# Sparse attention in units of two: scores of both, two half dense products with a transposition each, then the values of both

## Chip, cores and metric

The kernel runs on one core of a Trainium2 chip. The metric is the device time of one execution in microseconds (us), as a median of several.

## What is computed

Two networks of two layers each, on 512 tokens of width 1024. The first network mixes tokens by a gated linear recurrence and by sparse attention, whose three branches (compressed, selected, window) are gated and summed; the second has convolution, retention, spatial gating, cross attention and a feed-forward part. Only the selected and the window branch of the first network are at issue. With 512 tokens both are causal attention over all keys, since 16 blocks of 64 tokens, or a window of 512, cover the whole sequence:

```python
o_slc = selected_attn(q_rope, k_sl, heads(vsl, KVH), sel, scale)
o_win = window_attn(q_rope, k_wn, heads(vwn, KVH), scale)
gates = jax.nn.sigmoid(ngate).reshape(B, T, 3, KVH, G).transpose(2, 0, 3, 4, 1)[..., None]
o_nsa = gates[0] * o_cmp + gates[1] * o_slc + gates[2] * o_win
y_nsa = o_nsa * jax.nn.silu(nz)
h = h + jnp.concatenate([y_hg, y_nsa], axis=-1) @ w_out[i]
```

There are 8 query heads of width 64, handled in 4 pairs j, and 4 tiles t of 128 query rows.

## The kernel before

Dense products run on TensorE in float32 split into a high and a low part: `acc_fm` (line 458) issues three matmuls of 512 columns for each of 8 tiles of 128 inputs (lines 463 to 465), the weights' high part `whi` made on ScalarE (line 425), the low part `wlo` on VectorE or GpSimd (line 427). The raw weights come by DMA on SyncE's queue. `lin_steps` yields between the first and the last 12 matmuls of such a product: a dense half. `first_fill` (line 751) is a generator of such halves: the gates nz, hgo and hz (tanh `th` on ScalarE, line 784, a multiplication on VectorE, line 789), then the per-layer products wpp (`pp`, line 865), with small steps of the compressed branch (`Sc`, `ptc`) and of the recurrence (`spr`, `O`, line 1166) between them. Splits of activations into high and low parts (`yh`, `yl`, `ph`, `pl`) are lines 510 and 511. `pump(n)` runs n steps of the generator, and `pump(99)` what is left.

`nsa_pairs` (line 1298) does the two branches with an order of TensorE's instructions that is written out by hand, while the scheduler places the instructions of the other engines. A unit is a pair j, a tile t and one or both branches; n = 128(t+1) keys. There are 24 units in a layer, six for each j: t = 3 for each branch, t = 2 for each branch, then t = 1 and t = 0 with both branches at once. Each unit has three parts:

- `probs`: for each of the two heads a PSUM bank S, six score matmuls (line 1317) and two masks (line 1319); on VectorE the row maxima (line 1326) and their product with the scale (line 1328); on ScalarE exp with a running sum (line 1333); then the reciprocal of the sums and the gate (lines 1337 to 1341), and the scale of P on VectorE for one head (line 1343) and on ScalarE for the other (line 1344).
- `turn`: transposes of P on TensorE into a bank pt for each head (line 1356), copied to PT by ScalarE (line 1361) for one head and by VectorE (line 1363) for the other.
- `values`: matmuls of PT with v into the bank "no" of the pair (line 1376); with t = 0 also the compressed branch (lines 1379 and 1380), after which VectorE multiplies the sum by its gate (line 1382), and it is split.

S, pt, no, spr, Sc and ptc share six PSUM banks (`XB`); the dense products have two (`LIN`). Step i of the loop (line 1391 on) issues the scores and masks of unit i, the transposes of unit i-2, a dense half where `APUMP[i]` (line 1112) is 1, and the values of unit i-3. `APUMP` has 0 at i = 8, 14 and 19. At the end `begin` issues the first 21 matmuls of the output product wout.

Of the kernel before, what the change touches and what calls it, by code (L numbers as in the profile page):

```python
# [339 lines left out]
class Kern:  # L340
# [768 lines left out]
        self.pump()  # L1109

    DEEP = 2
    APUMP = tuple(map(int, "1111111101111101111011111"))
    HPUMP = (1,) * 16

    def stat_cols(self, ps, sq, o, rhs):
# [182 lines left out]
    def nsa_pairs(self, l, begin):  # L1298

        nc = self.nc  # L1300
        mm = nc.tensor.matmul
        po = [None]

        def probs(j, t, bs):

            ts = slice(t * 128, (t + 1) * 128)
            n = 128 * (t + 1)
            nb = len(bs)
            nm, sm = self.small([128, 2, 2], "nm", bufs=4), self.small([128, 2, 2], "sm", bufs=4)
            Ss = [self.xbank("S") for _ in range(2)]  # L1310
            bb = slice(bs[0], bs[-1] + 1)
            os = [S[:, :nb * n].rearrange("p (b s) -> p b s", b=nb) for S in Ss]
            qh, ql = self.q1[j]

            for i, (x, k) in enumerate(((qh, self.kh), (ql, self.kh), (qh, self.kl))):
                for o, hs in zip(os, HALVES):
                    mm(o, lhsT=x[hs, ts], rhs=k[hs, bb, :n], start=i == 0, stop=False)
            for o in os:
                mm(o[:, :, n - 128:], lhsT=self.identb, rhs=self.c["causal"][:, None, :].to_broadcast([128, nb, 128]),
                   start=False, stop=True)  # L1320
            Ps = {}
            rq = self.rq[:, j, t]

            with self.tc.high_priority(offset=200):
                for hd in range(2):
                    nc.vector.tensor_reduce(nm[:, :nb, hd], Ss[hd][:, :nb * n].rearrange("p (u s) -> p u s", u=nb),
                                            axis=AX, op=OP.max, negate=True)
                nc.vector.tensor_tensor(nm[:, :nb], nm[:, :nb], rq[:, None, :].to_broadcast([128, nb, 2]), op=OP.mult)  # L1328
                for hd in range(2):
                    P = self.slot("P")  # L1330
                    for i, b in enumerate(bs):
                        c = slice(i * n, i * n + n)
                        nc.scalar.activation(P[:, c], Ss[hd][:, c], AF.Exp, scale=rq[:, hd:hd + 1], bias=nm[:, i, hd:hd + 1],  # L1333
                                             accum_out=sm[:, i, hd:hd + 1])
                        Ps[b, hd] = P[:, c]
                s = sm[:, :nb]
                nc.vector.tensor_scalar(s, s, 1e-30, 4.0, op0=OP.max, op1=OP.mult)
                nc.vector.reciprocal(s, s)
                o = j * 6 + 2 + bs[0] * 2
                g = self.gth[:, t, o:o + nb * 2].rearrange("p (b h) -> p b h", h=2)  # L1340
                nc.vector.scalar_tensor_tensor(s, g, 1.0, s, op0=OP.add, op1=OP.mult)
                for i, b in enumerate(bs):
                    nc.vector.tensor_scalar(Ps[b, 0], Ps[b, 0], sm[:, i, 0:1], None, op0=OP.mult)
                    nc.scalar.activation(Ps[b, 1], Ps[b, 1], AF.Copy, scale=sm[:, i, 1:2])
            return Ps

        def turn(t, bs, Ps):

            n = 128 * (t + 1)
            PTs = []  # L1350
            for hd in range(2):
                pt = self.xbank("pt")
                for k, b in enumerate(bs):
                    for i in range(t + 1):
                        s = slice(i * 128, (i + 1) * 128)
                        nc.tensor.transpose(pt[:, k * n + i * 128:k * n + (i + 1) * 128], Ps[b, hd][:, s], self.ident)
                PT = self.slot("PT")
                m = len(bs) * n
                with self.tc.high_priority(offset=200):
                    if hd:  # L1360
                        nc.scalar.activation(PT[:, :m], pt[:, :m], AF.Copy)
                    else:
                        nc.vector.tensor_copy(PT[:, :m], pt[:, :m])
                PTs.append(PT)
            return PTs

        def values(j, t, bs, PTs):
            ts = slice(t * 128, (t + 1) * 128)
            n = 128 * (t + 1)
            if t == TT - 1 and bs[0] == 0:  # L1370
                po[0] = self.xbank("no")
            for k, b in enumerate(bs):
                for i in range(t + 1):
                    for hd in range(2):
                        v = self.vt[i][:, b * 128 + hd * 64:b * 128 + hd * 64 + 64]
                        mm(po[0][hd * 64:hd * 64 + 64, ts], lhsT=v, rhs=PTs[hd][:, k * n + i * 128:k * n + (i + 1) * 128],
                           start=t == TT - 1 and b == 0 and i == 0, stop=False)
            if t == 0:
                mm(po[0], lhsT=self.vc[0], rhs=self.pc[j], start=False, stop=False)
                mm(po[0], lhsT=self.vc[1 + j % 2], rhs=self.pc[j], start=False, stop=True)  # L1380
                O = self.slot("on")
                nc.vector.tensor_tensor(O, po[0], self.nzg[j], op=OP.mult)
                self.yn.append(self.split(O, "y"))

        branches = [((0, 1),), ((0, 1),), ((0,), (1,)), ((0,), (1,))]
        units = [(j, t, bs) for j in range(4) for t in reversed(range(TT)) for bs in branches[t]]
        n = len(units)
        Ps = {}


        with self.tc.manual_schedule(engines={mybir.EngineType.PE}):
            PTs = {}
            for i in range(n + 3):
                if i < n:
                    Ps[i] = probs(*units[i])
                if 0 <= i - 2 < n:
                    PTs[i - 2] = turn(*units[i - 2][1:], Ps.pop(i - 2))
                if i <= n:
                    self.pump(self.APUMP[i])
                elif i == n + 1:  # L1400
                    self.pump(99)
                    begin()
                if i >= 3:
                    values(*units[i - 3], PTs.pop(i - 3))


    def second(self, l):
# [491 lines left out]
```

## Time and profile before

| | |
|---|---|
| median of 3 runs | 2663.74 us (2661.94 to 2664.14) |
| the profiled execution | 2664.12 us, span 2662.4 us |
| granted TensorE clock, mean | 0.997 |
| TensorE, VectorE, ScalarE, GpSimd busy | 99%, 58%, 43%, 19% |
| the chain that ended last | TensorE 92%, VectorE 5%, ScalarE 2% |
| the attention stage of layer 0, of layer 1 | 211 to 351 us, 649 to 790 us |

The engines' shares are means over a span with several stages. The list of waits says for what TensorE stood still, the timeline gives single instructions with their starts, so that a start less the start before it is the pitch; the ends of matmuls are modelled. Windows give the busy time of each engine in a stretch, and the clock that TensorE was granted there (1.00 is full).

### The profile page before, as it was taken

Reading aid. Unit: us, or ns where it says so; the run is one execution under the profiler, and the core shown is the slowest. Engines: PE = TensorE matmul, PEld = TensorE weight load, DVE = VectorE, ACT = ScalarE, POOL = GpSimd, SP = SyncE. Lnnn points to the kernel's source line nnn. Section 1 sums busy time; section 2 is a strip of 40 time slices with the busy share of each in tenths; the row PEclk is TensorE's granted clock in tenths of the full one; section 3 lists DMA queues with packets and bytes.
Section 4 is the critical chain, followed back from the end, with each engine's and each line's share of the span. In section 5 each row is a group of like instructions: output and inputs, shape, how many; then the busy total and the mean of one; then the engine's idle time right before and its main releaser. Section 6 shows DMA issues by size and latency. Waiting matters only on the chain.

```text
span 2662.4 us, 34660 instructions
## 1 busy us (share of the span) xinstructions
PE 2629.0 (99%) x13574; PEld 2187.3 (82%) x13574; DVE 1537.1 (58%) x2310; ACT 1138.8 (43%) x2017; POOL 498.7 (19%) x430
## 2 busy tenths in 40 slices
PE   9999999999999999999999999999999999999998
PEld 7897778888778888888888888888888888888887
DVE  6687657687665655545555443555555555544444
ACT  5666655575664533334443222343333444422223
POOL 1254311054421141211010000114111000100101
PEclk9999999999999999999999999999999999999999
DMA  4311123321113323334323333232333432333332
GB/s 168 110 41 48 48 72 103 102 67 49 48 55 95 97 78 106 100 95 127 111 72 95 95 94 102 92 107 81 94 104 95 127 119 64 95 95 97 94 100 88
DMA packets 71890, 241.79 MB, mean 91 GB/s; under 512 B 8496, under 2 KB 11824, under 8 KB 71728
## 3 DMA queue, kind: packets, MB, share of 16 engines
q1 hardware_dynamic: 70288, 234.86, 28.8%
q0 software_dynamic: 1440, 4.72, 0.5%
q8 instruction: 108, 1.77, 0.3%
q14 instruction: 54, 0.44, 0.0%
HBM read 237.45 MB, written 2.10 MB: 90 GB/s over the span
## 4 chain that ended last, share of the span: by engine, by line
PE 92%; DVE 5%; ACT 2%; issue 1%; POOL 0%; DMA 0%; SPq 0%; DVEq 0%; ACTq 0%; POOLq 0%
PE lin_w L464 9%; PE lin_w L463 9%; PE lin_w L465 9%; PE lin_xq L464 1%; PE lin_wpg L464 1%; PE lin_xq L465 1%; PE lin_ga L465 1%; PE lin_ga L463 1%; PE lin_wo L463 1%; PE lin_wy L463 1%; PE lin_gc L463 1%; PE lin_gb L463 1%; PE lin_xq L463 1%; PE lin_wy L465 1%; PE lin_gc L465 1%; PE lin_gb L465 1%
## 5 line engine op out<-in xcount | busy, mean ns | idle before, releaser
L425 ACT ACTIVATE whi<-wraw 128x1024 fp32r<-128x1024 f32 (+2 forms) x433 | 453.1, 1047 | 1081.9 <-issue 531.5
L427 DVE TENSOR_TENSOR wlo<-wraw,whi 128x1024 fp32r<-128x1024 f32 (+2 forms) x409 | 562.8, 1377 | 155.1 <-ACT whi L425 150.8
L465 PE MATMUL lin_w<-xh,wlo 128*128 128x512 f32 x704 | 273.9, 389 | 0.0
L464 PE MATMUL lin_w<-xl,whi 128*128 128x512 f32 x704 | 273.9, 389 | 0.0
L463 PE MATMUL lin_w<-xh,whi 128*128 128x512 f32 x704 | 273.9, 389 | 0.0
L1519 POOL TENSOR_TENSOR fa<-fa,fb 128x512 f32<-128x512 f32 x44 | 61.1, 1389 | 613.7 <-DVE fb L610 510.4
L463 PEld LDWEIGHTS lin_w<-xh,whi 128*128 128x128 f32 x704 | 132.1, 188 | 27.6
L464 PEld LDWEIGHTS lin_w<-xl,whi 128*128 128x128 f32 x704 | 132.1, 188 | 27.4
L465 PEld LDWEIGHTS lin_w<-xh,wlo 128*128 128x128 f32 x704 | 132.1, 188 | 27.4
L464 PE MATMUL lin_w<-fyl,whi 128*128 128x512 f32 (+1 forms) x366 | 139.9, 382 | 0.9 <-DVE fyl L511 0.9
L463 PE MATMUL lin_w<-fyh,whi 128*128 128x512 f32 (+1 forms) x366 | 139.6, 381 | 0.0
L465 PE MATMUL lin_w<-fyh,wlo 128*128 128x512 f32 (+1 forms) x366 | 139.4, 381 | 0.0
L610 DVE TENSOR_TENSOR fb<-lin_w,rs 128x512 f32<-128x512 f32 x44 | 30.4, 691 | 138.9 <-PE lin_w L465 138.9
L1333 ACT ACTIVATE P<-S,nm,qkst 128x512 f32<-128x512 f32 (+3 forms) x128 | 77.6, 615 | 59.1 <-DVE nm L1328 58.6
L568 POOL TENSOR_TENSOR nacc<-sq 128x512 f32<-128x512 f32 x11 | 17.2, 1563 | 452.8 <-ACT sq L562 452.8
L1529 DVE TENSOR_TENSOR h<-lin_w,h 128x512 f32<-128x512 f32 x40 | 27.7, 692 | 106.8 <-PE lin_w L465 106.8
L427 POOL TENSOR_TENSOR wlo<-wraw,whi 128x1024 fp32r<-128x1024 f32 x24 | 57.5, 2396 | 150.1 <-ACT whi L425 134.5
L464 PEld LDWEIGHTS lin_w<-fyl,whi 128*128 128x128 f32 x366 | 68.8, 188 | 15.2 <-DVE fyl L511 2.2
L1478 POOL TENSOR_TENSOR ga<-ga,gb 128x512 f32<-128x512 f32 x16 | 20.6, 1290 | 322.9 <-DVE gb L1477 322.9
L463 PEld LDWEIGHTS lin_w<-fyh,whi 128*128 128x128 f32 x366 | 68.8, 188 | 13.7
L465 PEld LDWEIGHTS lin_w<-fyh,wlo 128*128 128x128 f32 x366 | 68.8, 188 | 13.0
L568 POOL TENSOR_TENSOR nacc<-nacc,sq 128x512 f32<-128x512 f32 x33 | 56.2, 1704 | 102.3 <-DVE wlo L427 36.4
(609 smaller groups left out, 6863.4 us busy)
## 6 DMA issues: line engine op xcount, KB each, us to landing
wraw<-in_w SPq DMA_DIRECT2D x396, 512.0 KB, 3.5
wraw<-in_w SPq DMA_DIRECT2D x34, 448.0 KB, 3.2
wraw<-in_w SPq DMA_DIRECT2D x8, 256.0 KB, 5.4
mem<-in_mem POOLq DMA_DIRECT2D x8, 256.0 KB, 3.7
out<-y SPq DMA_DIRECT2D x8, 256.0 KB, 2.2
h<-in_x SPq DMA_DIRECT2D x7, 256.0 KB, 5.4
wraw<-in_w SPq DMA_DIRECT2D x4, 420.0 KB, 3.0
pin<-in_p POOLq DMA_DIRECT2D x4, 256.0 KB, 3.9
```

Source lines behind the costliest of these rows:

```text
L425: self.nc.scalar.activation(h[:, c], t[:, c], AF.Copy)
L427: eng.tensor_tensor(lo[:, c], t[:, c], h[:, c].bitcast(FT), op=OP.subtract)
L463: mm(ps[:, :n], lhsT=wh[:, k, :], rhs=xh[:, :n], start=a, stop=False)
L464: mm(ps[:, :n], lhsT=wh[:, k, :], rhs=xl[:, :n], start=False, stop=False)
L465: mm(ps[:, :n], lhsT=wl[:, k, :], rhs=xh[:, :n], start=False, stop=b)
L568: eng.tensor_tensor(acc[:, :n], self.nacc[:, :n], sq[:, :n], op=OP.add)
L610: self.nc.vector.tensor_tensor(t, ps, rs, op=OP.mult)
L1333: nc.scalar.activation(P[:, c], Ss[hd][:, c], AF.Exp, scale=rq[:, hd:hd + 1], bias=nm[:, i, hd:hd + 1], accum_out=sm[:, i, hd:hd + 1])
L1478: nc.gpsimd.tensor_tensor(gs[0], gs[0], gs[1], op=OP.add)
L1519: nc.gpsimd.tensor_tensor(a, a, b, op=OP.mult)
L1529: nc.vector.tensor_tensor(self.h[m], ps, self.h[m], op=OP.add)
```

## The change

The loop goes over rounds of two units. A round issues the scores of both units, then their four masks, then twice a dense half and the transposes of one unit of the round before, then the values of both units of the round before. `probs` is cut into `scores`, `masks` and the rest. A 13th round has no new units: it turns the 23rd unit, runs what is left of the fill and `begin`, turns the 24th, and does the values of both. `APUMP` becomes twenty 1 and then 1, 0, 1, 0; the first round runs two halves. In the changed kernel the maxima are line 1337, their product 1339, exp 1344, the sums 1348 to 1352, the scales of P 1354 (VectorE) and 1355 (ScalarE), the transposes 1367, the PT copies 1372 (ScalarE) and 1374 (VectorE), the values 1387 and the gate's product 1393.

```diff
--- before.py
+++ after.py
@@ -1109,7 +1109,7 @@
         self.pump()
 
     DEEP = 2
-    APUMP = tuple(map(int, "1111111101111101111011111"))
+    APUMP = (1,) * 20 + (1, 0) * 2
     HPUMP = (1,) * 16
 
     def stat_cols(self, ps, sq, o, rhs):
@@ -1301,12 +1301,11 @@
         mm = nc.tensor.matmul
         po = [None]
 
-        def probs(j, t, bs):
+        def scores(j, t, bs):
 
             ts = slice(t * 128, (t + 1) * 128)
             n = 128 * (t + 1)
             nb = len(bs)
-            nm, sm = self.small([128, 2, 2], "nm", bufs=4), self.small([128, 2, 2], "sm", bufs=4)
             Ss = [self.xbank("S") for _ in range(2)]
             bb = slice(bs[0], bs[-1] + 1)
             os = [S[:, :nb * n].rearrange("p (b s) -> p b s", b=nb) for S in Ss]
@@ -1315,9 +1314,21 @@
             for i, (x, k) in enumerate(((qh, self.kh), (ql, self.kh), (qh, self.kl))):
                 for o, hs in zip(os, HALVES):
                     mm(o, lhsT=x[hs, ts], rhs=k[hs, bb, :n], start=i == 0, stop=False)
-            for o in os:
+            return Ss
+
+        def masks(t, bs, Ss):
+            n = 128 * (t + 1)
+            nb = len(bs)
+            for S in Ss:
+                o = S[:, :nb * n].rearrange("p (b s) -> p b s", b=nb)
                 mm(o[:, :, n - 128:], lhsT=self.identb, rhs=self.c["causal"][:, None, :].to_broadcast([128, nb, 128]),
                    start=False, stop=True)
+
+        def probs(j, t, bs, Ss):
+
+            n = 128 * (t + 1)
+            nb = len(bs)
+            nm, sm = self.small([128, 2, 2], "nm", bufs=4), self.small([128, 2, 2], "sm", bufs=4)
             Ps = {}
             rq = self.rq[:, j, t]
 
@@ -1389,19 +1400,25 @@
 
 
         with self.tc.manual_schedule(engines={mybir.EngineType.PE}):
-            PTs = {}
-            for i in range(n + 3):
-                if i < n:
-                    Ps[i] = probs(*units[i])
-                if 0 <= i - 2 < n:
-                    PTs[i - 2] = turn(*units[i - 2][1:], Ps.pop(i - 2))
-                if i <= n:
-                    self.pump(self.APUMP[i])
-                elif i == n + 1:
-                    self.pump(99)
-                    begin()
-                if i >= 3:
-                    values(*units[i - 3], PTs.pop(i - 3))
+            for i in range(0, n + 2, 2):
+                now, old = units[i:i + 2], units[i - 2:i] if i else []
+                Ss = [scores(*u) for u in now]
+                for (j, t, bs), x in zip(now, Ss):
+                    masks(t, bs, x)
+                new = [probs(*u, x) for u, x in zip(now, Ss)]
+                PTs = []
+                for k, (j, t, bs) in enumerate(old):
+                    if i < n:
+                        self.pump(self.APUMP[i + k])
+                    elif k:
+                        self.pump(99)
+                        begin()
+                    PTs.append(turn(t, bs, Ps[k]))
+                if not old:
+                    self.pump(2)
+                for u, x in zip(old, PTs):
+                    values(*u, x)
+                Ps = new
 
 
     def second(self, l):
```

The rounds are named below by their first unit's number, 0, 2, ... 22.

On ScalarE, in the round of units 18 and 19 (both t = 3), this stood before (`P,sm<-S` are exps, `P<-P,sm` scales):

```order
L1333 ACTIVATE P,sm<-S,nm,qkst 128x512 x2
L1361 ACTIVATE PT<-pt 128x512
L425 ACTIVATE whi<-wraw 128x1024
L1344 ACTIVATE P<-P,sm 128x512
L784 ACTIVATE th<-lin_hz_3315 128x512
L510 ACTIVATE yh<-th 128x512
L1333 ACTIVATE P,sm<-S,nm,qkst 128x512 x2
L1361 ACTIVATE PT<-pt 128x256
```

and this stands there now:

```order
L425 ACTIVATE whi<-wraw 128x1024
L1344 ACTIVATE P,sm<-S,nm,qkst 128x512 x4
L1355 ACTIVATE P<-P,sm 128x512 x2
L784 ACTIVATE th<-lin_hz_3346 128x512
L510 ACTIVATE yh<-th 128x512
L1372 ACTIVATE PT<-pt 128x512
L865 ACTIVATE pp<-lin_wpp_3475 128x512
L865 ACTIVATE pp<-lin_wpp_3484 128x512
L1372 ACTIVATE PT<-pt 128x256
```

The weight split now stands ahead of the four exps, and the PT copies behind both scales, a gate's tanh and its split, the last one behind two `pp` as well.

On VectorE, in the round of units 12 and 13 (both t = 3), before (`nm<-S` are the maxima):

```order
L1326 TENSOR_REDUCE nm<-S 128x1 x2
L1328 TENSOR_TENSOR nm<-nm,qkst 128x2
L1363 COPY PT<-pt 128x512
L1337 TENSOR_SCALAR sm<-sm 128x2
L1338 RECIPROCAL sm<-sm 128x2
L1341 SCALAR_TENSOR_TENSOR sm<-gth,sm 128x2
L1343 TENSOR_SCALAR P<-P,sm 128x512
L1326 TENSOR_REDUCE nm<-S 128x1 x2
L1328 TENSOR_TENSOR nm<-nm,qkst 128x2
L1363 COPY PT<-pt 128x256
L1337 TENSOR_SCALAR sm<-sm 128x2
L1338 RECIPROCAL sm<-sm 128x2
```

and now:

```order
L1337 TENSOR_REDUCE nm<-S 128x1 x4
L1339 TENSOR_TENSOR nm<-nm,qkst 128x2 x2
L1348 TENSOR_SCALAR sm<-sm 128x2
L1349 RECIPROCAL sm<-sm 128x2
L1352 SCALAR_TENSOR_TENSOR sm<-gth,sm 128x2
L1354 TENSOR_SCALAR P<-P,sm 128x512
L1348 TENSOR_SCALAR sm<-sm 128x2
L1349 RECIPROCAL sm<-sm 128x2
L1352 SCALAR_TENSOR_TENSOR sm<-gth,sm 128x2
L1354 TENSOR_SCALAR P<-P,sm 128x512
L1374 COPY PT<-pt 128x512
L1374 COPY PT<-pt 128x256
```

All four maxima and both products come first, and the two PT copies, which stood between a unit's product and its sums, come last.

On TensorE, at the end of the stage, from the masks of the last unit on, before:

```order
L1319 LDWEIGHTS identb
L1319 MATMUL S<-c_causal,identb 128x256
L1319 LDWEIGHTS identb
L1319 MATMUL S<-c_causal,identb 128x256
L1356 MATMUL pt<-c_ident,P 128x128 x6
L463 MATMUL lin_wpp_3696<-ph,whi 128x512
L464 MATMUL lin_wpp_3696<-pl,whi 128x512
L465 MATMUL lin_wpp_3696<-ph,wlo 128x512
```

where the 12 matmuls of a dense half (wpp) begin that ends before the values; and now, from the masks of the last unit but one on:

```order
L1324 LDWEIGHTS identb
L1324 MATMUL S<-c_causal,identb 128x256
L1324 LDWEIGHTS identb
L1324 MATMUL S<-c_causal,identb 128x256
L1367 MATMUL pt<-c_ident,P 128x128 x12
L1387 MATMUL no<-PT,vt 64x128 x12
L1367 MATMUL pt<-c_ident,P 128x128 x8
L463 MATMUL lin_wout_3746<-yh,whi 128x512
```

The turns of units 20 and 21 follow the masks of 22 and 23 with no dense half between, then the values of both, the turn of unit 22 and the matmuls of wout.

## Rows read from the trace of the kernel before

**Rows 1.** Page, part 1: busy us (share of the span) xinstructions of each engine
```profile
PE 2629.0 (99%) x13574; PEld 2187.3 (82%) x13574; DVE 1537.1 (58%) x2310; ACT 1138.8 (43%) x2017; POOL 498.7 (19%) x430
```

**Rows 2.** Waits of TensorE, whole span: line waited for, us, times, longest us
```profile
PE S L1317 <- ACT P L1333: 8.4, 6, 3.3
PE ptc L1258 <- DVE sm L1341: 2.5, 2, 1.3
PE pt L1356 <- DVE PT L1363: 1.9, 2, 1.0
PE pt L1356 <- ACT P L1333: 1.6, 2, 0.8
```

**Rows 3.** Timeline of TensorE: start us, us, engine line op out<-in xcount [idle before]
```profile
280.69 0.49 PE L1317 MATMUL S<-kh,q1h 64*128 64x512 f32 x2
281.02 0.39 PE L1317 MATMUL S<-kh,q1l 64*128 64x512 f32 x2
281.25 0.40 PE L1317 MATMUL S<-kl,q1h 64*128 64x512 f32 x2
281.58 0.29 PE L1319 MATMUL S<-c_causal,identb 128*128 128x128 bf16 x2
281.70 1.04 PE L1356 MATMUL pt<-c_ident,P 128*128 128x128 f32 x8
282.50 0.48 PE L463 MATMUL lin_hz<-xh,whi 128*128 128x512 f32 x1
...
285.44 0.88 PE L1376 MATMUL no<-PT,vt 128*64 128x128 f32 x12
```

**Rows 4.** Groups of VectorE, 211 to 352 us: xcount | busy us, mean ns | idle
```profile
L1326 DVE TENSOR_REDUCE nm<-S 128x1 f32<-128x512 f32 x16 | 10.3, 681 | 2.5 <-PE S L1319 2.5
...
L1363 DVE COPY PT<-pt 128x512 f32<-128x512 f32 x12 | 8.2, 682 | 0.0
...
L1328 DVE TENSOR_TENSOR nm<-nm,qkst 128x2 f32<-128x2 f32 x16 | 5.3, 332 | 0.2
...
L1326 DVE TENSOR_REDUCE nm<-S 128x2 f32<-128x256 f32 x8 | 3.0, 416 | 0.8 <-PE S L1319 0.8
...
L511 DVE TENSOR_TENSOR pl<-pin,ph 128x512 fp32r<-128x512 f32 x2 | 2.4, 1218 | 0.0
```

**Rows 5.** Groups of ScalarE in the same stretch
```profile
L1333 ACT ACTIVATE P<-S,nm,qkst 128x512 f32<-128x512 f32 x16 | 12.3, 772 | 11.2 <-DVE nm L1328 11.2
...
L425 ACT ACTIVATE whi<-wraw 128x1024 fp32r<-128x1024 f32 x11 | 11.6, 1057 | 0.1
...
L1333 ACT ACTIVATE P<-S,nm,qkst 128x256 f32<-128x256 f32 x16 | 8.8, 561 | 9.6 <-DVE nm L1328 9.6
...
L1344 ACT ACTIVATE P<-P,sm 128x384 f32<-128x384 f32 x8 | 4.9, 616 | 2.6 <-DVE sm L1341 2.6
```

**Rows 6.** Timeline of TensorE where values follow a turn directly
```profile
292.40 1.04 PE L1356 MATMUL pt<-c_ident,P 128*128 128x128 f32 x8
293.38 0.66 PE L1376 MATMUL no<-PT,vt 128*64 128x128 f32 x8
```

**Rows 7.** Timeline of TensorE, VectorE and ScalarE: hand-overs of a 384-wide unit
```profile
295.87 0.28 PE L1319 MATMUL S<-c_causal,identb 128*128 128x128 bf16 x2
...
296.14 0.56 DVE L1326 TENSOR_REDUCE nm<-S 128x1 f32<-128x384 f32 x1
...
298.18 0.15 DVE L1328 TENSOR_TENSOR nm<-nm,qkst 128x2 f32<-128x2 f32 x1
...
298.43 0.67 ACT L1333 ACTIVATE P<-S,nm,qkst 128x384 f32<-128x384 f32 x1 [0.39 <-DVE nm L1328]
```

**Rows 8.** Windows: us, busy (x) of PE, PEld, DVE, ACT, POOL, PEclk, DMA, GB/s
```profile
324.50:327.00 2.50, 2.50 (x14) 2.12 (x15) 1.67 (x6) 1.59 (x4) 0.21 (x1) 0.60 0.00 0
327.00:329.00 2.00, 2.00 (x9) 1.66 (x8) 1.02 (x5) 1.79 (x6) 0.00 (x0) 0.64 0.00 0
762.30:768.00 5.70, 5.61 (x21) 4.69 (x22) 3.03 (x12) 3.69 (x10) 0.29 (x1) 0.50 0.00 1
```

## The prediction

> **What bounds the kernel now.** The page's list of engines comes first: TensorE is busy 2629.0 of 2662.4 us [rows 1], so time falls only where TensorE issues less or waits less, and rises as soon as it waits more. The list of what TensorE waited for, over the whole span, says how little is left to win in the stage that the change touches: scores waiting for a bank that the exp still reads 8.4, a compression transpose 2.5, transposes waiting for a PT copy 1.9 and for an exp 1.6, together 14.4 us in both layers [rows 2]. The stage runs from about 211 to 351 us and again from 649 to 790.
>
> The timeline of TensorE shows why the waits are so short [rows 3]. A unit is values, scores, masks, a transposition of the unit two back, a dense half. A dense half lasts 2.94 us (282.50 to 285.44). Scores are read two periods later, PT one period later, so the softmax, split over VectorE and ScalarE, has two dense halves to run under. The rows of VectorE and ScalarE give what that softmax costs [rows 4, 5]: per 512-wide unit two maxima of 681 ns, a multiplication of 332, then two exps of 772, a scale on each engine (616 for 384 columns on ScalarE) and two PT copies (682 on VectorE). In between, in the engines' own order, stand weight splits (1057 ns on ScalarE) and splits of up to 1218 ns (pl).
>
> **The change, part by part.** The number of matmuls, transposes, copies, exps and transfers is the same, so the busy time is not changed; what moves is the order. Write u, v for the two units whose scores a round computes, x, y for those it turns and sums, and M for the start of its first mask. TensorE's times in a round of 512-wide units are then: masks to M+0.5, first dense half to about M+3.5, turn of x 0.8 (281.70 to 282.50 [rows 3]), second half to M+7.3, turn of y, values at about M+8.
>
> (a) Switches. TensorE pays at each change of kind: the first pair of score matmuls after values takes 0.33 (280.69 to 281.02) where the next takes 0.23 (281.02 to 281.25), the last pair before the masks 0.33 too, so 0.10 each. A dense half has 12 matmuls of 512 columns, 2.76 us at 0.23; it takes 2.94, so 0.09 for each of its two ends [rows 3]. Turn straight to values takes 0.98 (292.40 to 293.38) where a turn before a dense half takes 0.80 (281.70 to 282.50) [rows 3, 6], so 0.18. Two units cost 2 x (0.10 + 0.10 + 0.09 + 0.09) = 0.76 now. A round costs 0.10 + 0.10 + 0.09 + 0.18 = 0.47 plus three switches that no row shows (mask to dense, dense to turn twice), bounded by 0 and 0.2 each; I take 0.05, nearest to the mask-to-turn step, which shows none (281.58 to 281.70 for two masks). That is 0.14 saved in each of 24 rounds, 3.5 us; the ends are 7 saved and 7 lost. The Trainium skill, TensorEngine Tiling (Array Packing), Key Properties, says that changing the tiling mode drains TensorE. That speaks for this change, which halves the runs of 64-row scores and 64-column values; by the rows such a change costs 0.10, the same as turn to dense, where no tile shape changes.
>
> (b) The exps start later. VectorE now does the four maxima of u and v before the first multiplication (its order shows all four, then both multiplications). The hand-overs are 0.27 from the first mask to the maximum (295.87 to 296.14) and 0.10 from the multiplication's end to the exp [rows 7]. So nothing is ready for ScalarE until M + 0.3 + 4 x 0.68 + 0.33 + 0.1, about M+3.4 for 512-wide units, and with 256- and 384-wide ones M+2.6 to M+3.0; now it is two maxima, M+2.1. The transposes of x need banks. Of the six, four hold S, one the sum "no", one is left, and in most rounds the second or the first half of the turn must take a bank that u's exp has just left.
>
> (c) Splits go ahead of the exps. In ScalarE's order the weight split (whi) stands ahead of the four exps in rounds 6, 12 and 18. It waits for TensorE's dense half to let go of the previous weights at about M+3.0 and takes 1.06 [rows 5], so u's first exp ends and is handed over at M + 4.1 + 0.77 + 0.1, about M+5.0, its second at M+5.8. TensorE wants the first bank at M+3.5 in round 6: it waits 1.4, transposes 0.4, and waits 0.35 for the second, 1.75 in all. In 12 and 18 the first half has the free bank, and the second waits 1.1 to 1.5.
>
> (d) PT copies come last. They stand at the end of both engines' pieces, behind the scales, th, ph, pl, yl; and the values follow y's turn directly, with no dense half between. Round 14 is the worst: ScalarE has one exp, whi to M+4.4, three exps of 0.67 to M+6.4, then two scales, th and the first ph, each about 0.6, to M+8.8 [rows 5, 7]. VectorE then needs two pl of 1.22, a yl, taken as long as the copy, and a PT copy of 0.68 [rows 4]: M+12.6 with every piece at its mean; I take M+12, since whi and th may start earlier. TensorE stands ready at M+8: 4.1. The same in 18 (two pp ahead of the last copy) 2.15, in 12 0.75.
>
> (e) The last rounds have too little dense work. Round 22 has none: after its masks at M+0.5 it turns x at once. Its bank comes free after maxima 2 x 0.68 + 2 x 0.42, a multiplication, two exps of 0.56: M + 0.3 + 2.2 + 0.33 + 0.1 + 1.1 + 0.1 = M+4.1 against M+1.0, a wait of 3.1 [rows 4, 5, 7]; the next transposes and the tail wait 1.1 and 0.95 more. Round 20 has one half: 1.15 and 3.15. Now both dense halves of wpp stand there and no wait is seen.
>
> Walked through like this, each round from its own M, one layer waits in rounds 2 to 22 for 4.0, 2.25, 1.75, 0.55, 2.55, 2.25, 4.1, 3.95, 3.65, 4.3 and 5.15: 34.5, so 69 in both. These are my sums and not rows; rounds 2, 4, 10 and 16 wait for exps and copies as in (c) and (d), at other widths. The waits of today go: 14.4. The sum is 69 - 14.4 - 3.5 = 51.
>
> (f) The clock. Behind the two longest waits of today (3.3 us [rows 2]) the granted clock of TensorE reads 0.60, then 0.64 for 2 us, and in layer 1 0.50 for 5.7 us [rows 8], the lower of its two levels (1.2 of 2.4 GHz) or between the two. That is 1.0 + 0.7 = 1.7 us lost and 2.8 lost, 4.5 together. The change removes these two waits and adds about three near or over 3 us in each layer, so 6 x 2.25 - 4.5 = +9 at most; on the other hand a slow or waiting TensorE lets the other two engines catch up, and the next wait shrinks. I set the two against each other.
>
> Transfers: the weight loads issued on SP and the few on POOL are the same and move by a few places; each was landed long before its split, as no wait in [rows 2] names a transfer. I cost this at nothing; its cover is the same dense stream.
>
> **The number.** The profiled execution is 2664.12 us, span 2662.4 and 1.7 around it, 0.4 above the median 2663.74 of three. 2664.1 + 51 = 2715 us.
>
> **The rivals.** First, milder: VectorE and ScalarE catch up during each wait so that later rounds are half as bad. Stalls 34.5 - 14.4 - 3.5 = +17, 2681 us. For it: VectorE is at 58% and ScalarE at 43% over the span, and my rounds don't carry slack over. Against: the waits in (c) and (e) start from TensorE's own events, so no slack elsewhere shortens them. Chance 0.20.
>
> Second, faster: the place is the bank for the turn of x after the first dense half. If u's exp ends before M+3.5 in most rounds, and the copies before M+8, TensorE never waits; then the 14.4 go, with 4.5 for the clock and 3.5 for switches: 2664.1 - 22.4 = 2642 us. The point that decides is whether the first exp begins before M+2.7 and no split stands before it. For it: the longest waits of today stand behind step 14 of the old loop, whose entry in the table is 0, so that a unit passes without a dense half; two halves in each round would cure that. Against: the four maxima alone reach M+3.0 and the order of ScalarE has whi in front. Chance 0.10. Half of it with some of the waits would end near no change.
>
> Third, the clock: if waits over 3 us follow each other so closely that the clock stays at its lower level, four more long stretches a layer cost as much as the one at 0.50, 8 x 2.8 = 22: 2737 us. For it: both long waits of today lowered the clock [rows 8]. Against: it came back within 2 to 8 us, and the rounds with the longest waits are the last four. Chance 0.12.
>
> That the change doesn't do what it says can be left out: the order shows the pairs in all 24 rounds.
>
> **How the numbers follow.** Forecast 0.54, at 2690 to 2730; milder 0.20; clock 0.12; faster 0.10; no change 0.04. A measurement of this kernel tells about 0.2% (5 us) from none. Faster by more: 0.10; within: 0.04; slower: 0.86. The range reaches from the milder case with switches at their good end (2664 + 17 - 4 = 2677, less 2 of clock) to stalls 30% above my sum (90 - 14.4 - 3.5 = 72) with the clock's 9: 2675 to 2745.
>
> **What would show it.** In the list of TensorE's waits: transposes waiting for the exp of the same round (line 1367 for line 1344) with 20 to 40 us, the values (line 1387) for the PT copies 15 to 30, and hardly any scores waiting for an exp. In the timeline, a wait of 3 us directly behind the masks of the last round with no dense half. The stage of layer 0 lasting some 165 us instead of 140, the same in layer 1, nothing outside. Granted clock under 1.00 in windows behind the long waits. I am wrong if the stage waits less than today, if exps begin before M+2.5, or if the waits lie on weight transfers.

## The result and the profile after

The changed kernel takes 2737.06 us in the median of four runs (2736.84 to 2738.8) against 2663.71 of before. The ratio is 1.0275, with a 95% interval of 1.0264 to 1.0287: 73 us slower, inside the range that was forecast (2675 to 2745) and 22 us above the forecast number.

The page's list of engines [rows 1] shows that the other engines do the same work as before, while TensorE is busy 19.6 us longer, with the same 13574 matmuls:

```profile
PE 2648.6 (97%) x13574; PEld 2210.5 (81%) x13574; DVE 1539.0 (56%) x2310; ACT 1138.4 (42%) x2017; POOL 498.2 (18%) x430
```

The list of TensorE's waits over the whole span (line waited for, us in total, times, longest; it answers to [rows 2]) shows the larger part:

```profile
PE no L1387 <- DVE PT L1374: 30.0, 16, 6.2
PE pt L1367 <- ACT P L1344: 16.4, 12, 2.8
PE ptc L1258 <- DVE sm L1348: 6.9, 2, 3.4
PE lin_wpp L463 <- DVE th L789: 5.7, 2, 2.8
PE no L1387 <- ACT pp L865: 5.3, 2, 2.6
PE no L1387 <- ACT PT L1372: 2.5, 7, 0.5
```

With two of 1.1 and 0.6 that are not shown (scores for `Pc`, wpp for `pp`) these are 68.5 us in the two layers, against 15.4 before (14.4 in [rows 2] and 1.0 of wpp). That is 53.1 more; with the 19.6 of busy time it makes 72.7, and the two profiled spans differ by 72.8 (2735.2 less 2662.4). The whole loss is therefore named: 53 us of waits and 20 us of longer busy time, which the windows below show to be slower matmuls. Scores waiting for an exp, the largest wait of before, is gone.

Where the waits stand, the timeline of TensorE shows for layer 0 (start, us, what starts, idle time before it and what ended it); layer 1 repeats these waits within 0.05 us:

```profile
231.56 0.66 PE L1258 MATMUL ptc<-c_ident,Pc 128*128 128x128 f32 x2 [3.44 <-DVE sm L1348]
...
254.15 1.45 PE L1387 MATMUL no<-PT,vt 128*64 128x128 f32 x12 [2.47 <-DVE PT L1374]
...
263.05 1.42 PE L1367 MATMUL pt<-c_ident,P 128*128 128x128 f32 x8 [1.28 <-ACT P L1344]
...
325.59 3.68 PE L1387 MATMUL no<-PT,vt 128*64 128x128 f32 x32 [6.20 <-DVE PT L1374]
...
342.06 1.94 PE L1387 MATMUL no<-PT,vt 128*64 128x128 f32 x24 [3.86 <-DVE PT L1374]
...
356.45 0.61 PE L463 MATMUL lin_wpp<-ph,whi 128*128 128x512 f32 x1 [2.83 <-DVE th L789]
...
372.15 4.14 PE L1387 MATMUL no<-PT,vt 128*64 128x128 f32 x32 [2.64 <-ACT pp L865]
...
381.58 0.55 PE L1367 MATMUL pt<-c_ident,P 128*128 128x128 f32 x3 [2.75 <-ACT P L1344]
```

The reader is to see two main kinds: values (L1387) that wait for PT copies, and transposes (L1367) that wait for an exp of the same round. Two more stand beside them. The 3.44 us at 231.56 are a compression transpose in round 2; on VectorE the four maxima stand ahead of the softmax that makes its `Pc`, on ScalarE a weight split, and one short instruction of that softmax took 1.66 us (see the last section). The 2.83 us at 356.45 are a dense half in round 18 whose bank VectorE has yet to read out (`th`). Before, [rows 2] had one wait of 3.3 us a layer; now there are seven of 2.4 us and more.

The windows behind such waits (us, busy (x) of PE, PEld, DVE, ACT, POOL, then PEclk, DMA share, GB/s; they answer to [rows 8]) show what made the matmuls slower:

```profile
232.00:236.00 4.00, 4.00 (x16) 3.52 (x15) 3.64 (x14) 2.49 (x5) 0.00 (x0) 0.50 0.28 105
263.00:267.00 4.00, 3.85 (x20) 3.12 (x21) 3.00 (x9) 3.73 (x9) 1.73 (x1) 1.00 0.27 61
296.00:299.00 3.00, 3.00 (x30) 2.21 (x29) 0.25 (x1) 0.03 (x1) 0.00 (x0) 1.00 0.42 142
326.00:329.00 3.00, 3.00 (x32) 2.87 (x28) 0.05 (x1) 0.00 (x0) 0.00 (x0) 0.50 0.03 5
343.00:346.00 3.00, 3.00 (x22) 2.28 (x20) 0.00 (x0) 0.00 (x0) 0.10 (x1) 0.51 0.02 5
357.00:360.00 3.00, 3.00 (x12) 2.10 (x10) 0.94 (x2) 0.77 (x2) 2.82 (x5) 0.50 0.00 0
373.00:376.00 3.00, 3.00 (x30) 2.89 (x26) 0.00 (x0) 0.05 (x1) 0.00 (x0) 0.50 0.03 5
```

Behind the waits of 3.44, 6.20, 3.86, 2.83 and 2.64 us (windows from 232, 326, 343, 357 and 373) the granted clock is at or next to the lower level (0.50 of full, 1.2 GHz). Behind those of 1.28 and 1.00 (263 and 296) it stays at 1.00. Taking busy time times the part of the clock that is missing, in windows of 1 us over both stages, 27.0 us are lost to it, against 4.9 in the kernel before. What is left of the busy time, 2648.6 - 27.0 against 2629.0 - 4.9, is 2.5 us less than before.

### The profile page after: what moved, and what is told of

Its sections match the earlier page's. It is cut to its first block, busy times and chain, and to the rows that moved or that the text cites. A ratio compares the mean times of both kernels' runs of the same rounds, so it can differ in the third digit from the quotient of the medians.

```text
span 2735.2 us, 34653 instructions
## 1 busy us (share of the span) xinstructions
PE 2648.6 (97%) x13574; PEld 2210.5 (81%) x13574; DVE 1539.0 (56%) x2310; ACT 1138.4 (42%) x2017; POOL 498.2 (18%) x430
## 4 chain that ended last, share of the span: by engine, by line
PE 89%; ACT 5%; DVE 4%; issue 1%; POOL 1%; DMA 0%; SPq 0%; ACTq 0%; DVEq 0%; POOLq 0%
PE lin_w L464 9%; PE lin_w L463 9%; PE lin_w L465 9%; ACT P L1344 2%; PE no L1387 1%; ACT whi L425 1%; PE lin_xq L464 1%; PE lin_wpg L465 1%; PE lin_xq L465 1%; PE lin_ga L463 1%; PE lin_wo L465 1%; PE lin_wy L463 1%; PE lin_gc L463 1%; PE lin_gb L463 1%; PE lin_ga L465 1%
## 5 line engine op out<-in xcount | busy, mean ns | idle before, releaser
L1387 PE MATMUL no<-PT,vt 128*64 128x128 f32 x640 | 57.6, 322 | 37.9 <-DVE PT L1374 30.0
L1387 PEld LDWEIGHTS no<-PT,vt 128*64 128x64 f32 x640 | 46.0, 162 | 47.6 <-DVE PT L1374 20.9
L1337 DVE TENSOR_REDUCE nm<-S 128x1 f32<-128x512 f32 (+2 forms) x96 | 51.0, 594 | 54.5 <-PE S L1324 54.5
L463 PEld LDWEIGHTS lin_w<-fyh,whi 128*128 128x128 f32 x366 | 68.8, 188 | 13.6
```

The source lines that it names most:

```text
L463: mm(ps[:, :n], lhsT=wh[:, k, :], rhs=xh[:, :n], start=a, stop=False)
```

## Experiments

All changes are made to the changed kernel unless said. "Waits" are those of the list above, for both layers.

**Masks behind each unit's scores.** The first unit's softmax can begin while TensorE still does the second unit's scores.

```diff
-                Ss = [scores(*u) for u in now]
-                for (j, t, bs), x in zip(now, Ss):
-                    masks(t, bs, x)
+                Ss = []
+                for j, t, bs in now:
+                    Ss.append(scores(j, t, bs))
+                    masks(t, bs, Ss[-1])
```

> The masks of a unit follow its own scores, so the first unit's maxima can start 0.7 us earlier, under the second unit's scores, and its product and exps no longer stand behind the second unit's maxima. Nothing else changes. Theory A, step (b) (a late start of the exps is part of the waits): transposes waiting for exps fall from 16.4 in both layers to 8 to 13, the values' waits by 1 to 4, the time to 2722 to 2732 us. Rival (the exps wait for the weight split or end too late anyway): 2734 to 2741 us, with 2 to 4 us for the added switches.

Measured: 2717.14 us, ratio to before 1.0201 (1.0184 to 1.0218), 20 us faster than the change. The transposes' waits for an exp fall from 16.4 to 6.0, and all that is left of them stands in round 22; the values' waits fall by 4. Round 6 on ScalarE shows why (first the change, then this run):

```profile
261.18 1.06 ACT L425 ACTIVATE whi<-wraw 128x1024 fp32r<-128x1024 f32 x1 [8.01 <-issue]
262.15 0.76 ACT L1344 ACTIVATE P<-S,nm,qkst 128x512 f32<-128x512 f32 x1
```
```profile
258.18 0.78 ACT L1344 ACTIVATE P<-S,nm,qkst 128x512 f32<-128x512 f32 x1 [5.80 <-DVE nm L1339]
...
258.95 0.77 ACT L1344 ACTIVATE P<-S,nm,qkst 128x512 f32<-128x512 f32 x1
...
259.71 0.77 ACT L1344 ACTIVATE P<-S,nm,qkst 128x512 f32<-128x512 f32 x1
...
260.46 0.77 ACT L1344 ACTIVATE P<-S,nm,qkst 128x512 f32<-128x512 f32 x1
...
261.22 1.06 ACT L425 ACTIVATE whi<-wraw 128x1024 fp32r<-128x1024 f32 x1
```

In the change the weight split went first and u's first exp began 4.0 us after the first mask (258.11); here the four exps are through before the split begins. Both parts of the theory on the exps, the late start (b) and the split ahead of them (c), are taken away by this one edit, so the run doesn't divide them. For the short waits of rounds 6, 12 and 18 VectorE's row of the change does, as an estimate:

```profile
260.78 0.28 DVE L1339 TENSOR_TENSOR nm<-nm,qkst 128x2 f32<-128x2 f32 x2
```

The first of the two products is done at about 260.94, so with the hand-over of 0.10 the exp could have begun at 261.04, 2.9 us after the first mask. It began at 262.15, behind the split, so the split has about 1.1 of the 1.28 us; rounds 12 and 18 read alike (1.09 of 1.29 and 1.06 of 1.24). The gain is larger than forecast.

**Three weight buffers**, meant to test (c) alone.

```diff
-    NSLOT = 42
-    RAW, HLB = 4, 2
+    NSLOT = 40
+    RAW, HLB = 3, 3
```

> Three buffers for split weights instead of two (one raw weight buffer and two of 42 tile slots given up for the room, in the whole kernel). The weight split no longer waits for TensorE's running dense half, so it is done before the exps need ScalarE. Theory A, step (c): the waits of 1.28, 1.29 and 1.24 us in rounds 6, 12 and 18 fall under 0.5, the waits for exps to 8 to 12 in both layers, the time to 2722 to 2732 us, if the rest of the kernel doesn't mind the rooms. Rival (the four maxima set the start of the exps alone): those three waits stay over 1.0, and 2734 us or more.

Measured: 2733.29 us (1.0258, 1.0243 to 1.0273). The three waits stay (1.28, 1.28 and 1.24 us), but the run decides nothing, for the edit didn't do what it was to do: with a third buffer the kernel makes the split of one weight further ahead, which again goes into the buffer of the product that has just ended. The split of round 6 begins at 260.99, when TensorE leaves its first dense half, as in the change. So no run shows what (c) costs by itself; the estimate above rests on rows alone.

**The second unit's values one round later.** Each PT copy of a second unit then has scores, masks and a dense half to run under.

```diff
+            late = []
...
                     PTs.append(turn(t, bs, Ps[k]))
+                    if k == 0 and late:
+                        values(*late.pop())
...
-                for u, x in zip(old, PTs):
-                    values(*u, x)
+                if old:
+                    values(*old[0], PTs[0])
+                    late.append((*old[1], PTs[1]))
...
+            values(*late.pop())
```

> The values of a round's second unit are issued one round later, behind the first turn, so each PT copy has a dense half to run under; nothing else is changed. Theory A (the missing cover of the PT copies is the largest part): values waiting for PT fall from 19 to about 3 us a layer, transposes waiting for exps stay at 8 to 11, and the clock drops behind the values' waits go; 2690 to 2703 us. Rival B (too much work on VectorE and ScalarE): the waits move to the transposes, 2725 us or more.

Measured: 2708.01 us (1.0163, 1.0148 to 1.0178), 29 us faster than the change. The values' waits fall from 37.8 to about 18:

```profile
PE no L1387 <- DVE PT L1374: 17.6, 6, 4.4
PE pt L1367 <- ACT P L1344: 14.4, 10, 2.8
```

That is the largest gain of a single edit, and the waits did not move to the transposes, so VectorE and ScalarE have room for the work; it is the order that held them up. It falls short of the 2690 to 2703 expected: three waits a layer stay, the longest 4.40 us in round 14.

**The second dense half behind both turns.**

```diff
                     if i < n:
-                        self.pump(self.APUMP[i + k])
+                        if k == 0:
+                            self.pump(self.APUMP[i])
...
                 if not old:
                     self.pump(2)
+                elif i < n:
+                    self.pump(self.APUMP[i + 1])
```

> The second dense half of a round moves from between the two turns to behind both, ahead of the values. Theory A (the values wait for PT copies because nothing stands between turn and values): the 19 us a layer of values waiting for PT fall to under 6; the second unit's transposes come 3 us earlier after the masks, so their waits for exps rise from 8.4 to 15 to 22 us a layer; together 2725 to 2745 us. Rival B (VectorE and ScalarE have more work in a round than TensorE, whatever the order): the sum of waits stays within 10% and so does the time, and the values go on waiting for PT by over 12 us a layer.

Measured: 2730.09 us (1.025, 1.0232 to 1.0267).

```profile
PE pt L1367 <- ACT P L1344: 34.8, 34, 2.8
PE no L1387 <- DVE PT L1374: 11.4, 3, 5.1
...
PE no L1387 <- ACT pp L865: 5.3, 2, 2.6
```

The one dense half covers either the exps or the copies: the transposes' waits double, the values' fall from 37.8 to some 17, which is less than half, but over the 12 that were expected. All waits of the stage together fall only from 68.5 to 63.6, and that they would stay within 10% was the rival's forecast. Against the rival speak the values' waits, some 8.5 us a layer where it wanted over 12, and the run with late values above.

**Dense halves kept for the end.**

```diff
-    APUMP = (1,) * 20 + (1, 0) * 2
+    APUMP = tuple(map(int, "111111101010111111111111"))
```

> Three dense halves are kept back (the second halves of rounds 6, 8 and 10 are left out), so that the last two rounds have both. Theory A (cover is missing everywhere, the dense work is only shifted): the waits of rounds 20 and 22, 7.7 us a layer, fall to 2 to 4, and rounds 6, 8 and 10 gain 2 to 3 us each; 2730 to 2745 us. Rival C (only the end of the stage is short of dense work): 2715 to 2722 us.

Measured: 2721.58 us (1.0213, 1.0198 to 1.0228), 15 us faster: the rival's range, at its end, and not the theory's. In layer 0 round 22 still waits 2.80 us (4.08 in the change), no longer for exps but for a bank of the dense products, which `pp` on ScalarE has yet to read. Rounds 18 and 20 wait 2.25 and 2.08 us instead of 4.07 and 3.58. The gate and the splits of round 14 come one round later with the dense halves, and the long wait with them: round 14 waits 0.5 us instead of 6.20, round 16 waits 5.69 instead of 3.86. Of the three rounds that gave a half away round 6 waits 3.4 us instead of 1.3 and round 10 2.6 instead of 1.25, but round 8 only 0.4 instead of 1.35. So dense work was not equally short everywhere: a half is worth more in the last rounds than in these.

**The splits on GpSimd.** Line 511's `pl`, two instructions ahead of the PT copies of round 14, goes from VectorE to GpSimd.

```diff
-        self.nc.vector.tensor_tensor(lo, src, h.bitcast(FT), op=OP.subtract)
+        (eng or self.nc.vector).tensor_tensor(lo, src, h.bitcast(FT), op=OP.subtract)
...
-                px.extend(self.split(s, "p") for s in pin)
+                px.extend(self.split(s, "p", eng=nc.gpsimd) for s in pin)
```

> The low part of the split that stands ahead of the PT copies in round 14 (two instructions, 1.24 us each on VectorE) goes to GpSimd; the result is the same. Theory A, step (d) (the PT copies stand behind other work on VectorE): the wait of 6.20 us in round 14 falls to 3.5 to 4.5, the time by 4 to 6 us to 2731 to 2733. Rival B (the wait is for something else, or GpSimd slows VectorE as much): 2735 to 2739 us.

Measured: 2735.76 us (1.0267, 1.0251 to 1.0282), no gain; the wait in round 14 is 5.73 us instead of 6.20. VectorE has 2.5 us less to do in that round, but its next split, which now runs beside GpSimd's, takes longer (start, us):

```profile
321.96 1.26 POOL L511 TENSOR_TENSOR pl<-pin,ph 128x512 fp32r<-128x512 f32 x1
323.18 2.15 POOL L796 TENSOR_TENSOR th<-th,O 128x128 f32<-128x128 f32 x4
```
```profile
319.97 0.68 DVE L789 SCALAR_TENSOR_TENSOR th<-th,lin_hz 128x512 f32<-128x512 f32 x1
321.96 1.81 DVE L511 TENSOR_TENSOR yl<-th,yh 128x512 fp32r<-128x512 f32 x1 [1.31 <-ACT yh L510]
323.69 1.27 DVE L1374 COPY PT<-pt 128x512 f32<-128x512 f32 x2
```

`yl` takes 1.81 us, where it took 0.94 in the change (323.91), and it has to wait until 321.96 for `yh`, which stands behind two `ph` on ScalarE. That GpSimd's instruction is what lengthens `yl` is argued from the two rows and not shown by a run of its own.

**Dummy products while TensorE waits**, to price the clock alone. Ahead of the values of rounds 4, 14, 16 and 20 TensorE runs 8, 22, 14 and 8 products that nobody reads; the sums are as before.

```diff
+                warm = {4: 8, 14: 22, 16: 14, 20: 8}.get(i, 0)
                 for u, x in zip(old, PTs):
+                    if warm and (i > 4 or u is old[1]):
+                        ps = self.ps.tile([128, 512], FT, name="warmth", tag="lin", bufs=self.LIN)
+                        for _ in range(warm):
+                            mm(ps[:, :128], lhsT=self.ones, rhs=self.ones, start=True, stop=True)
+                        warm = 0
                     values(*u, x)
```

> TensorE runs dummy products of 128 columns (0.21 us each: 8, 22, 14, 8) ahead of values that wait in rounds 4, 14, 16 and 20, into a bank of the dense products that nobody reads; the computation is the same. Theory D (the lower granted clock behind waits of 2.5 us and more costs 13 us a layer): behind these four waits the clock stays at 1.00, 1.6 to 2.5 us each are won, 2720 to 2726 us. If the clock is of no account: 2735 to 2739 us.

Measured: 2730.15 us (1.0247, 1.0232 to 1.0262), 7 us faster with more for TensorE to do. The windows that were at 0.50 above are at full clock:

```profile
326.00:329.00 3.00, 3.00 (x38) 2.48 (x35) 0.45 (x1) 0.00 (x0) 0.00 (x0) 1.00 0.00 0
343.00:346.00 3.00, 3.00 (x21) 2.25 (x18) 2.07 (x4) 0.00 (x0) 0.00 (x0) 1.00 0.00 0
```

By the same sum as before 13.6 us are lost to the clock instead of 27.0, so 13.4 less, but the time falls by only half of that, into neither of the two ranges. Where the other half went, the rows show. In round 4 the dummies end before the copies do: 1.7 us of clock come back, and the round, from its first mask to that of the next, is 1.5 us shorter. In rounds 14, 16 and 20 they begin late, behind a bank that another engine still reads, take 0.235 us each (5.18 for 22) where 0.21 was reckoned, and end late. In round 14 (start, us):

```profile
319.98 5.18 PE L1424 MATMUL warmth<-ones 128*128 128x128 f32 x44 [1.93 <-DVE th L789]
325.09 1.97 PE L1387 MATMUL no<-PT,vt 128*64 128x128 f32 x32
```
```profile
323.48 1.27 DVE L1374 COPY PT<-pt 128x512 f32<-128x512 f32 x2
```

The first of the two copies ends at 324.16, so the values began some 0.9 us later than they could have; in rounds 16 and 20 it is 0.8 and 0.5 us, by the same reading. That is about 4.4 us in both layers, an estimate, of the 6.6 that are missing; the rest stays open. That a slow TensorE lets VectorE and ScalarE catch up, so that the next wait is shorter, isn't seen: rounds 6 and 18, which follow a stretch that was slow in the change and is at full clock here, last 13.81 and 13.82 us, 16.74 and 16.78 in layer 0. So, where the rows let it be read, nearly all of the loss to the clock was time lost.

**Three edits together, twice.** Late values, kept halves and `pl` on GpSimd:

> Three of the edits together: values of the second unit one round later, three dense halves kept for the last rounds, the two splits on GpSimd. If the three add up (29 and 15 us measured singly, 5 expected): 2688 to 2693 us. If they cover the same waits: 2698 us or more.

Measured: 2682.86 us (1.0068, 1.0053 to 1.0083), below both ranges and better than the sum: 29 + 15 + 1 from 2737 would be 2692. Then early masks in place of the GpSimd splits, and the half of round 6 taken from round 12 instead:

```diff
+    APUMP = tuple(map(int, "111111111010101111111111"))
```

> The pairs with three repairs: masks behind each unit's scores, values of the second unit one round later, three dense halves kept for the end (now left out in rounds 8, 10 and 12; round 6, where the last such run still waited 2.70 us, has both again). The splits stay on VectorE. If the waits named by the theory are all there is: 29 us of stage waits are left in the run with late values and kept halves, of which the early masks take some 10 and the half in round 6 some 5, with 4 us of clock; 2660 to 2670 us, so that the pairs cost nothing against the kernel before. If pairs wait by their nature (four maxima and four exps in a row): 2675 us or more.

Measured: 2674.35 us (1.004, 1.0026 to 1.0054). The time lies between the two ranges. The values wait 2.5 us in all and the transposes for an exp 2.8; what stands first in the list is the compressed branch and wpp:

```profile
PE ptc L1258 <- DVE Pc L1287: 5.8, 4, 2.7
PE lin_wpp L463 <- ACT pp L865: 4.3, 5, 1.8
PE pt L1367 <- ACT P L1344: 2.8, 6, 0.8
PE ptc L1258 <- ACT whi L425: 2.4, 2, 1.2
```

So 63 of the 73 us come back by orders of the same work. Four maxima and four exps in a row don't by themselves make TensorE wait, but the pairs don't win either: this version is still 11 us behind the kernel before. Of the 10.2 us between the two spans 4.7 are waits of the stage (20.2 against 15.5), the clock gives 1.7 back, and 7 are busy time (2634.5 against 2629.0) that the clock doesn't explain; no run says what it is.

**The table of the kernel before.** In the first run step 14 gets its dense half back from step 10; in the second step 19 does; in the third the zeros stand at 8, 10 and 12.

```diff
-    APUMP = tuple(map(int, "1111111101111101111011111"))
+    APUMP = tuple(map(int, "1111111101011111111011111"))
...
+    APUMP = tuple(map(int, "1111111101011101111111111"))
...
+    APUMP = tuple(map(int, "1111111101010111111111111"))
```

> The kernel before, with one entry of its table changed: the dense half that is missing in step 14 is put there, and step 10 goes without one. The longest wait of before (3.3 us a layer, behind step 14) and the clock's fall behind it (1.7 and 3.2 us) go, if step 10 can spare its half: 2651 to 2657 us. If step 10 needs its half as much, the wait only moves: 2660 to 2668 us.

> The kernel before with the dense half put back into step 19, where the wait of 3.3 us really stands (the step turns a unit of t = 0 and goes from the transposes straight to the values), and taken from step 10; the table has 0 at 8, 10 and 14. If a missing dense half is what makes the wait: the 3.3 us and the clock's loss behind it (1.7 and 3.1 us) go in both layers, 2651 to 2657 us, faster than both kernels. If step 10 or 14 then waits as long: 2661 to 2668 us.

> As the run with step 19 filled, but step 14 has its half too and step 12 goes without; zeros at 8, 10 and 12. If the early steps have room and the late ones not: the wait behind step 19 is gone and the waits of 0.97 us at step 13 to 15 shrink, 2649 to 2656 us. If three missing halves so close together are too many: waits of over 1 us in steps 9 to 14, 2658 us or more.

Measured: 2665.99 us (1.001, 1.0001 to 1.0019), 2652.61 us (0.9956, 0.9943 to 0.9968) and 2655.82 us (0.9967, 0.9955 to 0.9979). The first gained nothing (it is 2.5 us slower): the wait of 3.26 us was still there, in a step that goes from the transposes of a t = 0 unit straight to the values, which is step 19. Filled there, the wait is gone, step 10 pays for it with 0.77 us, and no window of either stage is under full clock (the first run's line, then the second's):

```profile
PE S L1317 <- ACT P L1333: 10.0, 8, 3.3
```
```profile
PE S L1317 <- ACT P L1333: 3.4, 6, 0.8
```

With zeros at 8, 10 and 14 this kernel beats both, by 12 us and by 84: 6.8 us of waits and 4.9 of clock. With zeros at 8, 10 and 12 it is 3.2 us slower than that, inside the range forecast for it.

## Why the prediction held, and where it was off

- **Busy work and (a).** Held. Counts are equal, and without the clock's share TensorE is busy 2.5 us less, against 3.5 forecast for the switches (24 times 0.14 is 3.4). The Trainium skill, TensorEngine Tiling (Array Packing), Key Properties, has a drain at each change of tiling mode, of which the change has fewer of some kinds and adds others; the 2.5 us are the balance, and no run divides it.
- **(b) and (c), exps late and behind the split.** Held in sum: the early masks take away every wait for an exp but that of round 22. Of the three short waits in rounds 6, 12 and 18 the split has about 1.1 us each, by the estimate above; no run tests it alone. The exp could have begun at M+2.9 where M+3.4 was forecast (four maxima took 2.48 us and not 2.72, and the product 0.16 where 0.33, a mean of unlike ones, was put), and the first exp of round 6 began at M+4.0 where M+4.1 was. In all, transposes waited 16.4 us for exps, less than the 20 to 40 that were to show it.
- **(d), PT copies last.** Held and was the largest part, larger than forecast: values waited 37.8 us in both layers where 15 to 30 were to show it, and issuing one unit's values later is worth 29 us. In round 14 the forecast was 4.1 us and the trace has 6.20; about half of the difference is in the last section.
- **(e), no dense work at the end.** Held in place: the first bank in round 22 was to cost 3.1 us and cost 2.75.
- **The sum of the waits.** 34.5 us a layer were forecast, 34.3 measured. The rounds from 2 to 22, forecast and measured (rows of the timeline): 4.0 and 4.0, 2.25 and 2.7, 1.75 and 1.3, 0.55 and 1.35, 2.55 and 1.25, 2.25 and 1.9, 4.1 and 6.2, 3.95 and 3.9, 3.65 and 4.1, 4.3 and 3.6, 5.15 and 4.1. Single rounds were off by up to 2 us, both ways, so that the sums meet within 0.2 us is luck. Round 2 met its number by another cause, the compression transpose, and 2.83 of round 18's 4.1 us are the dense half that waits for a bank, which the walk doesn't have.
- **(f), the clock.** This is the term that was mis-sized, and it is the whole 22 us between 2715 and 2737. The prediction counted three waits a layer near or over 3 us that lower the clock, at 9 us at most, and set them at nothing against the shorter waits behind them. Three a layer are over 3 us, as counted, but the four of 2.47 to 2.83 us lowered it too: 27.0 us were lost less the 4.9 of before, and TensorE's busy time rose by 19.6. And there was nothing to set against it: in the run with dummy products rounds behind a faster TensorE last as long as before, and where the dummies didn't overrun, 1.5 of 1.7 us came back. So 53 of waits and 20 of busy time simply add, and setting the one against the other was the mistake.
- **The rivals.** The third, the clock, forecast 2737 and gave the number, in part by luck: it reckoned eight stretches of 2.8 us on a clock that stays low, and the trace has fourteen of 1.5 to 2.9 us, behind each of which the clock was back at 1.00 within 3.5 to 6.5 us. The milder one fell, since the waits were all there and no catching up is seen. The faster one fell at the point named: the first exp of round 6 begins at M+4.0, with a split before it. Its argument also had the place wrong: the longest wait of before stands behind step 19 of the old table and not step 14, as two runs show, one by doing nothing.

## What to carry to other kernels

When units of a software pipeline are grouped, ask of each copy and each exp which work of the bottleneck engine stands between it and its reader: the same work in the same amount cost 73 us, and 63 of them came back once values no longer followed their copies directly, a group's maxima no longer stood ahead of its first exp, and the last rounds had dense work again. Put filler work where the reader would wait, and find that place in the trace rather than in the table: one entry moved was worth 12 us, and another, moved by the table alone, nothing. A long wait of TensorE cost more than its length here, because the matmuls behind it ran at a lower clock: look at the granted clock there, and add its loss to the waits.

## What was not expected of the hardware

- **A short VectorE instruction behind a long one of GpSimd.** In round 14 of the change VectorE's first instruction on the sums of the exps, 128 x 2, takes 1.82 us where the next of its kind takes 0.16. It ends with GpSimd's weight split (316.44 + 2.39 = 318.83):

```profile
316.44 2.39 POOL L427 TENSOR_TENSOR wlo<-wraw,whi 128x1024 fp32r<-128x1024 f32 x1 [4.77 <-ACT whi L425]
```
```profile
317.04 1.82 DVE L1348 TENSOR_SCALAR sm<-sm 128x2 f32<-128x2 f32 x1 [2.36 <-ACT P L1344]
...
319.63 0.16 DVE L1348 TENSOR_SCALAR sm<-sm 128x2 f32<-128x2 f32 x1
```
```profile
319.35 0.61 ACT L1355 ACTIVATE P<-P,sm 128x384 f32<-128x384 f32 x1 [1.03 <-DVE sm L1352]
```

 It isn't the only one. In each layer of the change six such instructions of VectorE, on 128 x 2 to 128 x 8 sums, take 0.6 to 1.8 us, and each ends 0.03 us after the end of an instruction of GpSimd, five of them after a weight split. The kernel before has the like on others: a product of the maxima (256.92, 128 x 2) takes 1.65 us instead of 0.15 and ends 0.02 us after a weight split. Summed over layer 0, VectorE's instructions that are over 0.3 us longer than is usual for them take some 13 us too long in either kernel, an estimate; in the change part of it stands where TensorE waits, which the prediction doesn't have. In round 2 of layer 0 it is the 128 x 8 instruction of the compressed branch (228.86 + 1.66 = 230.52, the split 228.15 + 2.34 = 230.49), some 1.5 of the 3.44 us that the transpose waits:

```profile
228.86 1.66 DVE L1282 TENSOR_SCALAR csm<-csm 128x8 f32<-128x8 f32 x1
```
```profile
228.15 2.34 POOL L427 TENSOR_TENSOR wlo<-wraw,whi 128x1024 fp32r<-128x1024 f32 x1 [7.76 <-PE Sc L1269]
```

 The Trainium skill, SBUF — State Buffer, Summary: rules for kernel authors, says that when both engines run, and VectorE is in a two-port mode, or has two inputs in SBUF while GpSimd's instruction reads SBUF, the later of the two instructions is blocked until the first has finished. These rows agree in the end they show; which of the two conditions held they don't tell. In round 14 ScalarE stood still for 1.03 us until the sums came, so about 1.0 of the 2.1 us by which that round was longer than forecast is this, an estimate; the other half stays open. All of it is read from rows, and no run took the GpSimd split away.
- **The clock behind waits.** In the two stages of the change every wait of 2.4 us and more was followed by a granted clock near 0.5 for some microseconds, 1.5 to 2.9 us lost each; none of 1.3 us and less was. [rows 8] had only the two of 3.3 us. The other runs show that the length alone doesn't tell: in the pairs with all three repairs (2674.35 us) the 2.74 us ahead of the compression transpose in layer 1 were followed by full clock, and with early masks alone 1.24 us in round 2 of layer 0 were followed by 0.50.
